# A hybrid decoder trunk on one core: the first phase laid out anew, with its loads in order of need, two modulation columns by matmuls, and a fixed engine order

## The chip, the cores and the metric

The program runs on one core of one Trainium2 chip. The metric is the device time of one execution, in microseconds (us), lower is better. The engines of the core work side by side, each through its own list of instructions in order: TensorE (PE in the profile, PEld for its weight loads) multiplies, VectorE (DVE) and ScalarE (ACT) do the elementwise work, SyncE (SP) issues nearly all transfers. They wait for one another through semaphores.

## What is computed

Two decoder layers over 512 tokens of width 1024. Each sub-layer is normalised and modulated by a shift and a scale that come from a conditioning vector `c`. The change touches only the start of layer 0: the modulation columns, the first norm, and the first projections that read its output.

```python
def rmsnorm(t, g):
    y = tf * lax.rsqrt(jnp.mean(tf * tf, axis=-1, keepdims=True) + EPS)
    return (y * g.astype(jnp.float32)).astype(t.dtype)

def modulate(t, g, shift, scale):
    return rmsnorm(t, g) * (1.0 + scale[:, None, :]) + shift[:, None, :]
...
c_act = jax.nn.silu(c)
for i in range(DEPTH):
    mod = c_act @ ada_w[i] + ada_b[i]
    sh1, sc1, g1, sh2, sc2, g2 = jnp.split(mod, 6, axis=-1)
    h = modulate(x, norm_mix[i], sh1, sc1)
    ...
        y = gla_mixer(h, gla_w_in[j], ...)      # proj = h @ w_in; q, k, v, r, glr
    x = x + g1[:, None, :] * y
    h = modulate(x, norm_ffn[i], sh2, sc2)
    x = x + g2[:, None, :] * swiglu(h, ffn_w_in[i], ffn_w_out[i])
```

## The kernel before

Activations lie transposed: eight tiles `x[k]` of 128 features by 512 tokens. A product is made in three matmuls (`mm3`, lines 172 to 177): both operands are split into a rounded high part and a low rest, and high times high, high times low and low times high are added up in PSUM. A weight unit of 128 by 1024 numbers is loaded into `raw` (line 155), copied to its high part `wh` by ScalarE (line 161), and VectorE makes the low part `wl` (line 169). The pool `wp` has three buffers each of `raw`, `wh` and `wl`.

A modulation column (128 of the 6144 outputs of `c_act @ ada_w`, `ada` at line 128) is made by VectorE: a tile `adaw` of 128 by 1024 weights is loaded (line 132), multiplied with `cact`, which holds silu(c) on every partition, and summed along the row (`junk`, line 136); the bias is added into `mod` (line 138). `gain` (line 143) makes the factor `gs` from a scale column. The pool for `adaw` has two buffers.

The first phase (lines 424 to 456) runs as follows.

- SP loads the eight tiles `x[k]`, with the row `crow` (the vector c) after the fourth. ScalarE's queue loads `kc` (an identity and a causal mask) and `cols` (biases and norm gains).
- TensorE spreads c over all partitions: two matmuls into `cb` (line 428) with one row of ones.
- ScalarE squares the `x[k]` (lines 261 and 264), VectorE adds the squares into `acc` (line 262). After the eighth square ScalarE makes `cact` from `cb` in two halves (line 434).
- `rstd_stats` (line 216): four matmuls with one output column each (`n_st`, line 225) sum `acc` over the partitions, and eleven small VectorE operations (lines 203 to 228, from `rs_v` to `rs_f`) make 1/rms. `rstd_spread` (line 234): four matmuls `n_bc` (line 240) bring it onto all partitions.
- `modulated` (line 267): `u` = x·gs·rstd on VectorE, `hh` = the rounded u + shift on ScalarE, `hl` the rest on VectorE.
- For each k the eight banks `ko` (the gate's small projection and seven of the eight head projections of q and k) receive 24 matmuls: 128 features of h[k] against the weight unit `gla_ko[k]`. All eight k make 192 matmuls, the phase's real work; the matmuls `gate` come behind them.

For k = 0 the order on TensorE, ScalarE and VectorE is written out by hand (`manual_schedule`). For k = 1 to 7 the framework's scheduler orders all engines, with one rule (line 450): the work of a column and weight unit k may not be issued before the low part `wl` of the unit before. SP's order is the scheduler's throughout. Each transfer also waits for the one eight transfers earlier on its queue of eight semaphores.

## Time and profile before

| What | Value |
|---|---|
| time, median of 3 runs | 1204.73 us (1204.16 to 1206.95) |
| the profiled execution, span from first to last instruction | 1203.1 us; the profile gives no other time for it |
| share of the span with a busy engine | PE 98%, weight loads 83%, DVE 61%, ACT 34% |
| instructions | 15359, of them 6010 matmul passes |
| DMA | 156.66 MB, mean 130 GB/s |
| first ten slices of the span (30.1 us each): PE busy, in tenths | 5 9 9 9 9 9 9 9 9 9 |
| the same for the DMA engines | 8 8 3 2 4 5 3 4 4 1 |

A busy share says little about a stage: matmuls are pipelined and their recorded ends overlap the next one's start. What ends last is read from the chain of waits, from the starts of successive instructions, and from what each engine's idle time ended with. The runs' median lies 1.6 us above the profiled span; what lies around the span is not resolved by the profile, so a difference worked out on the span is applied to the median as it stands. In the clock column of the table by stretches, 1.00 stands for full speed and 0.50 for half; it starts from the first event that the profiler recorded.

### The profile page before, as it was taken

How to read it: one execution, taken by the hardware profiler on the slowest of the kernel's cores; microseconds unless marked ns; L12 is line 12 of the kernel's file. 1: busy time of each engine (PE TensorE's matmuls, PEld its weight loads, DVE VectorE, ACT ScalarE, POOL GpSimd, SP SyncE). 2: the span in 40 equal slices, each digit the busy share in tenths (PEclk: the TensorE clock that was granted, in tenths of full speed). 3: DMA queues.
4: the chain of work that ended last, by engine and by line, in shares of the span. 5: the costliest groups of instructions: out<-in, count | busy, mean ns of one | idle time of the engine just before them, and what ended most of it. 6: DMA issues, size and time to landing. Idle time of an engine off the chain costs nothing.

```text
span 1203.1 us, 15359 instructions
## 1 busy us (share of the span) xinstructions
PE 1173.1 (98%) x6010; PEld 999.4 (83%) x6010; DVE 732.0 (61%) x1434; ACT 414.3 (34%) x652; POOL 15.9 (1%) x36
## 2 busy tenths in 40 slices
PE   5999999999999999999999999999999999999996
PEld 3788988899888888888899788989888888888886
DVE  6879788776665466846656778856433323333345
ACT  4271235343221223222334446634332223222331
POOL 0000000000000000000000022000000000000000
PEclk9999999999999999999999999999999999999998
DMA  8832453441574367547531123131333232333222
GB/s 283 266 98 105 170 179 127 134 160 53 193 262 142 113 243 251 152 158 246 182 114 45 57 66 106 35 124 34 96 98 103 91 103 85 92 105 105 83 76 71
DMA packets 47290, 156.66 MB, mean 130 GB/s; under 512 B 5601, under 2 KB 8033, under 8 KB 47218
## 3 DMA queue, kind: packets, MB, share of 16 engines
q1 hardware_dynamic: 45394, 153.38, 38.8%
q0 software_dynamic: 1536, 2.10, 0.8%
q8 instruction: 47, 0.77, 0.3%
q10 hardware_dynamic: 288, 0.21, 0.1%
q14 instruction: 25, 0.20, 0.1%
HBM read 151.47 MB, written 2.10 MB: 128 GB/s over the span
## 4 chain that ended last, share of the span: by engine, by line
PE 89%; DVE 6%; DMA 3%; ACT 1%; issue 1%; ACTq 0%; DVEq 0%
PE f L176 12%; PE f L177 12%; PE f L175 12%; PE op L175 9%; PE op L176 9%; PE op L177 9%; DMA adaw<-in_ada 2%; PE lv L541 2%; PE fg L176 2%; PE fg L177 2%; PE fg L175 2%; DVE junk L136 1%; PE v L175 1%; PE v L177 1%; PE v L176 1%; PE r L175 1%
## 5 line engine op out<-in xcount | busy, mean ns | idle before, releaser
L161 ACT CAST wh<-raw 128x1024 fp32r<-128x1024 f32 (+2 forms) x181 | 185.7, 1026 | 584.6 <-PE f L176 180.2
L169 DVE TENSOR_TENSOR wl<-raw,wh 128x1024 fp32r<-128x1024 f32 (+2 forms) x181 | 215.2, 1190 | 119.5 <-ACT wh L161 112.4
L175 PE MATMUL f<-hh,wh 128*128 128x512 f32 x640 | 249.2, 389 | 0.0
L176 PE MATMUL f<-hl,wh 128*128 128x512 f32 x640 | 249.2, 389 | 0.0
L177 PE MATMUL f<-hh,wl 128*128 128x512 f32 x640 | 249.2, 389 | 0.0
L175 PE MATMUL op<-acth,wh 128*128 128x512 f32 (+1 forms) x394 | 144.8, 368 | 0.0
L176 PE MATMUL op<-actl,wh 128*128 128x512 f32 (+1 forms) x394 | 144.5, 367 | 0.0
L177 PE MATMUL op<-acth,wl 128*128 128x512 f32 (+1 forms) x394 | 144.4, 367 | 0.0
L177 PEld LDWEIGHTS f<-hh,wl 128*128 128x128 f32 x640 | 120.1, 188 | 24.9
L176 PEld LDWEIGHTS f<-hl,wh 128*128 128x128 f32 x640 | 120.2, 188 | 24.9
L175 PEld LDWEIGHTS f<-hh,wh 128*128 128x128 f32 x640 | 120.1, 188 | 24.9
L136 DVE SCALAR_TENSOR_TENSOR junk<-adaw,cact 128x1024 bf16<-128x1024 f32 x96 | 117.1, 1220 | 12.7 <-DMA adaw<-in_ada 12.3
L284 DVE SCALAR_TENSOR_TENSOR x<-op,mod,x 128x512 f32<-128x512 f32 (+1 forms) x76 | 50.5, 665 | 119.2 <-PE op L177 119.1
L782 DVE TENSOR_TENSOR sg<-sg,f 128x512 f32<-128x512 f32 x40 | 27.5, 687 | 126.6 <-PE f L177 126.6
L176 PEld LDWEIGHTS op<-actl,wh 128*128 128x128 f32 x394 | 74.3, 189 | 12.2
L175 PEld LDWEIGHTS op<-acth,wh 128*128 128x128 f32 x394 | 74.3, 189 | 12.2
L177 PEld LDWEIGHTS op<-acth,wl 128*128 128x128 f32 x394 | 74.3, 189 | 12.1
L274 ACT ACTIVATE hh<-u,mod 128x256 fp32r<-128x256 f32 (+1 forms) x56 | 28.6, 536 | 56.5 <-DVE u L271 40.9
L262 DVE TENSOR_TENSOR acc<-acc,sq 128x512 f32<-128x512 f32 (+1 forms) x52 | 29.9, 576 | 17.5 <-ACT sq L261 17.2
L261 ACT ACTIVATE sq<-x 128x512 f32<-128x512 f32 (+1 forms) x45 | 23.6, 525 | 41.2 <-DVE x L284 38.5
L275 DVE SCALAR_TENSOR_TENSOR hl<-u,mod,hh 128x256 fp32r<-128x256 f32 (+1 forms) x56 | 27.9, 520 | 12.1 <-ACT hh L274 12.1
L784 DVE TENSOR_TENSOR actl<-sg,acth 128x512 fp32r<-128x512 f32 (+1 forms) x48 | 30.7, 641 | 0.8 <-ACT acth L783 0.5
(308 smaller groups left out, 1918.2 us busy)
## 6 DMA issues: line engine op xcount, KB each, us to landing
adaw<-in_ada SPq DMA_DIRECT2D x96, 512.0 KB, 4.1
raw<-in_ffn_in SPq DMA_DIRECT2D x80, 512.0 KB, 3.6
raw<-in_ffn_o SPq DMA_DIRECT2D x32, 448.0 KB, 3.3
raw<-in_ffn_o SPq DMA_DIRECT2D x16, 512.0 KB, 3.5
raw<-in_gla_ko SPq DMA_DIRECT2D x8, 512.0 KB, 4.5
raw<-in_gla_v SPq DMA_DIRECT2D x8, 512.0 KB, 3.6
raw<-in_gla_r SPq DMA_DIRECT2D x8, 512.0 KB, 3.6
raw<-in_gla_wo SPq DMA_DIRECT2D x8, 512.0 KB, 4.2
```

The source lines that it names most:

```text
L136: nc.vector.scalar_tensor_tensor(out=junk, in0=w, scalar=1.0, in1=cact, op0=ALU.mult, op1=ALU.mult, accum_out=acc)
L161: nc.scalar.copy(out=wh[:, :n], in_=raw[:, :n])
L169: ins = nc.vector.tensor_tensor(out=wl[:, :n], in0=raw[:, :n], in1=wh[:, :n].bitcast(F32), op=ALU.subtract)
L175: nc.tensor.matmul(ps, lhsT=ah, rhs=bh, start=start, stop=False)
L176: nc.tensor.matmul(ps, lhsT=ah, rhs=bl, start=False, stop=False)
L177: nc.tensor.matmul(ps, lhsT=al, rhs=bh, start=False, stop=stop)
L262: nc.vector.tensor_tensor(out=self.acc[:, c], in0=self.acc[:, c], in1=sq[:, c], op=ALU.add)
L274: nc.scalar.activation(out=hi[:, c], in_=u[:, c], func=AF.Identity, bias=sh)
L275: ins = nc.vector.scalar_tensor_tensor(out=lo[:, c], in0=u[:, c], scalar=sh, in1=hi[:, c].bitcast(F32), op0=ALU.add, op1=ALU.subtract)
L284: ins = nc.vector.scalar_tensor_tensor(out=x[k][:, c], in0=ps[:, c], scalar=mod[l][2 + 3 * j][:, k:k + 1], in1=x[k][:, c], op0=ALU.mult, o ...
L782: ins = nc.vector.tensor_tensor(out=sg[:, c], in0=sg[:, c], in1=pu[:, c], op=ALU.mult)
L784: nc.vector.tensor_tensor(out=lo[:, c], in0=sg[:, c], in1=hi[:, c].bitcast(F32), op=ALU.subtract)
```

## The change

It rewrites the first phase and leaves the rest of the program's instruction lists as they are, apart from the order of a few transfers just behind the phase.

- `crow` is loaded first, then the eight x, then for k = 0 and 1 the scale column, the shift column and the weight unit; in the loop, unit k+1 is requested at step k. SP's order is now written out too, for the whole phase.
- The sixteen `adaw` tiles of this phase land in a pool `first` of six buffers; the space is handed to the pool `att` behind the phase.
- TensorE begins with six matmuls `warm` of the identity against `kc`, whose result nobody reads.
- The two columns of k = 0 are made by TensorE (`ada_pe`): eight float32 matmuls of one output column each, from blocks that the host lays out transposed, against `ccol` (silu of c, one number a partition and block). The columns of k = 1 to 7 stay on VectorE.
- The eighth square is not added into `acc`; TensorE sums `acc` and the last `sq` in eight `n_st` matmuls.
- `cact` is made by ScalarE behind the fourth square and ahead of the fifth.
- For k = 1 to 7 the factor `gs` comes straight from the row sum in one operation, with `nb` = (1 + bias)·gain made once.
- TensorE, ScalarE and VectorE follow a written order for all eight k.

On TensorE, at the very start of the program (`am` is the bank of a column made by matmuls), before:

```order
L428 MATMUL cb<-crow,onesr 128x512 x2
L225 MATMUL n_st<-ones,acc 128x1 x4
L240 MATMUL n_bc<-kc,rs_f 128x128 x4
L447 MATMUL ko_230<-hh,wh 128x512
L447 MATMUL ko_231<-hh,wh 128x512
```

On TensorE at the same place, of the change:

```order
L453 MATMUL warm<-kc 128x256 x6
L456 MATMUL cb<-crow,onesr 128x512 x2
L226 MATMUL n_st<-ones,acc 128x1 x4
L226 MATMUL n_st<-ones,sq 128x1 x4
L477 MATMUL am<-ccol,adaw 128x1 x8
L241 MATMUL n_bc<-kc,rs_f 128x128 x4
L477 MATMUL am<-ccol,adaw 128x1 x8
L494 MATMUL ko_261<-hh,wh 128x512
```

Ten matmuls stood ahead of the first `ko`; now 36 do, and `cb` stands behind `warm`.

On ScalarE at the start of the program, before:

```order
L264 ACTIVATE acc<-x_83 128x512
L261 ACTIVATE sq<-x_84 128x512
L261 ACTIVATE sq<-x_85 128x512
L261 ACTIVATE sq<-x_86 128x512
L261 ACTIVATE sq<-x_87 128x512
L261 ACTIVATE sq<-x_88 128x512
L261 ACTIVATE sq<-x_89 128x512
L261 ACTIVATE sq<-x_90 128x512
L434 ACTIVATE cact<-cb 128x512 x2
```

On ScalarE at the same place, of the change:

```order
L265 ACTIVATE acc<-x_80 128x512
L262 ACTIVATE sq<-x_81 128x512
L262 ACTIVATE sq<-x_82 128x512
L262 ACTIVATE sq<-x_83 128x512
L468 ACTIVATE cact<-cb 128x512 x2
L262 ACTIVATE sq<-x_84 128x512
L262 ACTIVATE sq<-x_85 128x512
L262 ACTIVATE sq<-x_86 128x512
L470 ACTIVATE sq<-x_87 128x512
```

The two `cact` moved from behind the last square to ahead of the fifth.

On VectorE, from the end of the 1/rms chain (`rs_f`) into the first steps of the loop, before:

```order
L212 SCALAR_TENSOR_TENSOR rs_f<-rs_b,rs_o 128x4
L136 SCALAR_TENSOR_TENSOR junk,adac<-adaw,cact 128x1024
L138 TENSOR_TENSOR mod_0_109<-adac,cols 128x1
L271 SCALAR_TENSOR_TENSOR u<-x_83,gs_0_121,n_bc 128x512
L275 SCALAR_TENSOR_TENSOR hl<-u,mod_0_109,hh 128x512
L169 TENSOR_TENSOR wl<-raw,wh 128x1024
L136 SCALAR_TENSOR_TENSOR junk,adac<-adaw,cact 128x1024
L169 TENSOR_TENSOR wl<-raw,wh 128x1024
L138 TENSOR_TENSOR mod_1_110<-adac,cols 128x1
L136 SCALAR_TENSOR_TENSOR junk,adac<-adaw,cact 128x1024
```

On VectorE at the same place, of the change:

```order
L213 SCALAR_TENSOR_TENSOR rs_f<-rs_b,rs_o 128x4
L480 TENSOR_TENSOR mod_1_96<-am,cols 128x1
L147 SCALAR_TENSOR_TENSOR gs_0_107<-mod_1_96,cols 128x1
L480 TENSOR_TENSOR mod_0_95<-am,cols 128x1
L272 SCALAR_TENSOR_TENSOR u<-x_80,gs_0_107,n_bc 128x512
L276 SCALAR_TENSOR_TENSOR hl<-u,mod_0_95,hh 128x512
L170 TENSOR_TENSOR wl<-raw,wh 128x1024
L130 SCALAR_TENSOR_TENSOR junk,adac<-adaw,cact 128x1024
L499 TENSOR_SCALAR gs_0_107<-adac,cols,nb 128x1
L503 SCALAR_TENSOR_TENSOR u<-x_81,gs_0_107,rstd 128x512
L130 SCALAR_TENSOR_TENSOR junk,adac<-adaw,cact 128x1024
L139 TENSOR_TENSOR mod_0_95<-adac,cols 128x1
```

The row sum behind `rs_f` is gone; in its place the shift column `mod_0` waits for the second `am`, and `u` is queued behind it.

The diff, cut to its core (comments that it drops are left out):

```diff
+C_C = 148
+NC_COL = 156
...
-    att = ctx.enter_context(tc.tile_pool(name="att", bufs=2))
...
-    for k in range(KD):
-        nc.sync.dma_start(out=x[k], in_=t["x"][k])
-        if k == 3:
-            nc.sync.dma_start(out=crow[:1], in_=t["c"])
-    nc.scalar.dma_start(out=kc, in_=t["kc"])
-    nc.scalar.dma_start(out=cols, in_=t["cols"])
...
-    def ada(l, g, k):
-        n = g * KD + k
-        w = ap_.tile([P, D], F32, tag="adaw", name="adaw")
-        nc.sync.dma_start(out=w, in_=t["ada"][l * 48 + n])
+    def ada_load(l, g, k, pool):
+        w = pool.tile([P, D], F32, tag="adaw", name="adaw")
+        nc.sync.dma_start(out=w, in_=t["ada"][l * 48 + g * KD + k])
+        return w
+    def ada_dot(w):
         junk = ap_.tile([P, D], BF16, tag="junk", name="junk", bufs=1)
-        m = mod[l][g][:, k:k + 1]
         acc = sm.tile([P, 1], F32, tag="adac", name="adac")
         nc.vector.scalar_tensor_tensor(out=junk, in0=w, scalar=1.0, in1=cact,
                                        op0=ALU.mult, op1=ALU.mult, accum_out=acc)
+        return acc
+
+    def ada(l, g, k, w=None):
+        n = g * KD + k
+        m = mod[l][g][:, k:k + 1]
+        acc = ada_dot(ada_load(l, g, k, ap_) if w is None else w)
         nc.vector.tensor_tensor(out=m, in0=acc, in1=cols[:, C_ADAB + l * 48 + n:C_ADAB + l * 48 + n + 1],
                                 op=ALU.add)
...
-    with tc.manual_schedule(engines={PEM, ACTM, DVEM}):
-        cb = [bank("cb") for _ in range(2)]
-        for i in range(2):
-            nc.tensor.matmul(cb[i], lhsT=onesr, rhs=crow[:1, i * S:(i + 1) * S], start=True, stop=True)
-        nc.scalar.activation(out=cact[:, :1], in_=ones, func=AF.Silu)
-        ss = SumSq()
-        for k in range(KD):
-            ss.add(x[k])
-        for i in range(2):
-            nc.scalar.activation(out=cact[:, i * S:(i + 1) * S], in_=cb[i], func=AF.Silu)
-        ada(0, 1, 0)
-        gain(0, 0, 0)
-        y0 = rstd_stats(ss.acc, D, "n0")
-        w = wunit(t["gla_ko"][0], split_=False)
-        ada(0, 0, 0)
-        bc = rstd_spread(y0, None, "n0")
-        modulated(h[0], 0, 0, 0, bc)
-        nc.scalar.copy(out=rstd, in_=bc)
-        wunit_lo(w)
-        pko = [bank(f"ko{i}") for i in range(4)] + [abank(f"ko{i}") for i in range(4, 8)]
-        for n, (a, b) in enumerate(((0, 0), (0, 1), (1, 0))):
-            for i in range(8):
-                nc.tensor.matmul(pko[i], lhsT=w[a][:, i * P:(i + 1) * P], rhs=h[0][b], start=n == 0, stop=False)
-    for k in range(1, KD):
-        with tc.issue_after(last["w"]):
-            ada(0, 1, k)
-            ada(0, 0, k)
-            gain(0, 0, k)
-            w = wunit(t["gla_ko"][k])
-        modulated(h[k], k, 0, 0, rstd)
-        for i in range(8):
-            mm3(pko[i], sl(w, slice(None), slice(i * P, (i + 1) * P)), h[k], False, k == KD - 1)
+    def wload(src):
+        raw = wp.tile([P, 1024], F32, tag="raw", name="raw")
+        nc.sync.dma_start(out=raw, in_=src)
+        return raw
+
+    def wsplit(raw):
+        wh = wp.tile([P, 1024], F32R, tag="wh", name="wh")
+        wl = wp.tile([P, 1024], F32R, tag="wl", name="wl")
+        nc.scalar.copy(out=wh, in_=raw)
+        return wh, wl, raw
+
+    SPM = mybir.EngineType.SP
+    with tc.tile_pool(name="first", bufs=6) as first:
+        with tc.manual_schedule(engines={PEM, ACTM, DVEM, SPM}):
+            nc.scalar.dma_start(out=kc, in_=t["kc"])
+            nc.scalar.dma_start(out=cols, in_=t["cols"])
+            nc.sync.dma_start(out=crow[:1], in_=t["c"])
+            for k in range(KD):
+                nc.sync.dma_start(out=x[k], in_=t["x"][k])
+            ld = {}
+            for k in range(2):
+                ld[k] = ada_load(0, 1, k, first), ada_load(0, 0, k, first), wload(t["gla_ko"][k])
+            warm = abank("warm")
+            for i in range(6):
+                nc.tensor.matmul(warm[:, :256], lhsT=ident, rhs=kc, start=i == 0, stop=i == 5)
+            cb = [bank("cb") for _ in range(2)]
+            for i in range(2):
+                nc.tensor.matmul(cb[i], lhsT=onesr, rhs=crow[:1, i * S:(i + 1) * S], start=True, stop=True)
+            ccol = cst.tile([P, KD], F32, name="ccol")
+            nc.scalar.activation(out=ccol, in_=cols[:, C_C:C_C + KD], func=AF.Silu)
+
+            nb = cst.tile([P, KD], F32, name="nb")
+            nc.vector.scalar_tensor_tensor(out=nb, in0=cols[:, C_ADAB + KD:C_ADAB + 2 * KD], scalar=1.0,
+                                           in1=cols[:, C_NMIX:C_NMIX + KD], op0=ALU.add, op1=ALU.mult)
+            ss = SumSq()
+            for k in range(KD - 1):
+                ss.add(x[k])
+                if k == 3:
+                    for i in range(2):
+                        nc.scalar.activation(out=cact[:, i * S:(i + 1) * S], in_=cb[i], func=AF.Silu)
+            sq = R("sq")
+            nc.scalar.activation(out=sq, in_=x[KD - 1], func=AF.Square)
+            y0 = rstd_stats([ss.acc, sq], D, "n0")
+
+            def ada_pe(g):
+                w = ld[0][0 if g else 1]
+                am = abank("am")
+                for b in range(KD):
+                    nc.tensor.matmul(am[:, :1], lhsT=w[:, b * P:(b + 1) * P], rhs=ccol[:, b:b + 1],
+                                     start=b == 0, stop=b == KD - 1)
+                n = g * KD
+                nc.vector.tensor_tensor(out=mod[0][g][:, 0:1], in0=am[:, :1],
+                                        in1=cols[:, C_ADAB + n:C_ADAB + n + 1], op=ALU.add)
+
+            ada_pe(1)
+            gain(0, 0, 0)
+            w = wsplit(ld[0][2])
+            bc = rstd_spread(y0, None, "n0")
+            ada_pe(0)
+            modulated(h[0], 0, 0, 0, bc)
+            nc.scalar.copy(out=rstd, in_=bc)
+            wunit_lo(w)
+            pko = [bank(f"ko{i}") for i in range(4)] + [abank(f"ko{i}") for i in range(4, 8)]
+            for n, (a, b) in enumerate(((0, 0), (0, 1), (1, 0))):
+                for i in range(8):
+                    nc.tensor.matmul(pko[i], lhsT=w[a][:, i * P:(i + 1) * P], rhs=h[0][b], start=n == 0, stop=False)
+            for k in range(1, KD):
+                if k + 1 < KD:
+                    ld[k + 1] = ada_load(0, 1, k + 1, first), ada_load(0, 0, k + 1, first), wload(t["gla_ko"][k + 1])
+                wsc, wsh, raw = ld.pop(k)
+                nc.vector.tensor_scalar(out=gs_t[0][0][:, k:k + 1], in0=ada_dot(wsc),
+                                        scalar1=cols[:, C_NMIX + k:C_NMIX + k + 1], scalar2=nb[:, k:k + 1],
+                                        op0=ALU.mult, op1=ALU.add)
+                u = R("u")
+                nc.vector.scalar_tensor_tensor(out=u, in0=x[k], scalar=gs_t[0][0][:, k:k + 1], in1=rstd,
+                                               op0=ALU.mult, op1=ALU.mult)
+                w = wsplit(raw)
+                ada(0, 0, k, wsh)
+                sh = mod[0][0][:, k:k + 1]
+                hi, lo = h[k]
+                nc.scalar.activation(out=hi, in_=u, func=AF.Identity, bias=sh)
+                wunit_lo(w)
+                nc.vector.scalar_tensor_tensor(out=lo, in0=u, scalar=sh, in1=hi.bitcast(F32),
+                                               op0=ALU.add, op1=ALU.subtract)
+                for i in range(8):
+                    mm3(pko[i], sl(w, slice(None), slice(i * P, (i + 1) * P)), h[k], False, k == KD - 1)
+    att = ctx.enter_context(tc.tile_pool(name="att", bufs=2, reuse_waits="tile"))
...
+    for n in (0, KD):
+        d["ada"][n] = outer(aw[0][:, n * P:(n + 1) * P])[0]
+    put(C_C, f("c"))
```

## The prediction, made before the changed kernel was run

> **What bounds the kernel now.** I read the page first: PE is busy 98% of the span, and of its first ten slices only the first isn't full, so behind it the kernel runs at TensorE's own pace. A change to the first phase is worth what it moves the end of that phase. So I read the chain of waits from the start to the first `gate` (start, length, what):

> ```profile
> 11.04 0.64 ACT sq L261
> 11.71 0.70 DVE acc L262
> 12.46 1.88 PE n_st L225 x8
> 14.36 0.17 DVE rs_v L228
> ...
> 16.55 2.09 PE n_bc L240 x8
> 18.67 0.76 DVE u L271
> 19.45 0.73 ACT hh L274
> ...
> 38.40 6.28 DMA adaw<-in_ada
> ...
> 47.30 4.65 DMA adaw<-in_ada
> ...
> 53.23 4.50 DMA adaw<-in_ada
> ...
> 60.66 0.23 PE ko L177
> ...
> 70.20 0.23 PE ko L177
> 70.43 0.42 PE gate L175
> ```

> The phase has two parts. A head of one long dependence: last square, sum, `n_st`, eleven small operations, `n_bc`, `u`, `hh`. And a loop, where the chain runs through transfers of `adaw` again and again: two buffers are too few, and the column after next is requested only when one comes free. The last rows give TensorE's pace in the loop: 42 matmuls from 60.66 to 70.20, so 0.227 us each. The phase ends at 70.4. TensorE's timeline gives the loop's start:

> ```profile
> 6.18 3.75 PE L428 MATMUL cb<-crow,onesr 1*128 1x512 f32 x4 [6.18 <-DMA crow<-in_c]
> 20.22 3.78 PE L447 MATMUL ko<-hh,wh 128*128 128x512 f32 x8 [1.59 <-ACT hh L274]
> 23.80 2.12 PE L447 MATMUL ko<-hl,wh 128*128 128x512 f32 x8
> 25.76 1.97 PE L447 MATMUL ko<-hh,wl 128*128 128x512 f32 x8
> ```

> The loop lasts 70.4 − 20.2 = 50.2 us, and its 192 matmuls at 0.227 need 43.6. The reader should also see the first eight `ko` take 3.6 us (20.22 to 23.80) and the next eight 2.0: TensorE starts at half pace and doubles about 3.5 us later. So the whole head, `cb`, `n_st`, `n_bc`, ran at half pace, though the clock column says 1.00 there (it knows no event yet). The same small matmuls later in the program, at full pace:

> ```profile
> L225 PE MATMUL cq_st<-ones,acc x8: 249/250/271, 675.1 to 675.9; 128*128 128x1 f32 x8
> 681.90 1.13 PE L240 MATMUL cq_bc<-kc,rs_f 128*128 128x128 f32 x8
> ```

> Eight passes (a float32 matmul is two) start within 0.8 us: 0.11 a pass, against 1.88/8 = 0.23 in the head.

> **The change: the loop.** With six `adaw` buffers three columns' worth can be in flight, and each step needs three transfers of 512 KB. At the 358 GB/s of a well-filled stretch (its row stands below, at 102.57) that is 1.57 MB in 4.4 us, under the 5.45 of 24 matmuls. The requests lead: the scale column of k+3 goes out when that of k has been summed, some 14 us ahead of its use. So the starvation goes, and VectorE is late next. Its work for a step, by the starts in its timeline:

> ```profile
> 42.33 0.15 DVE L138 TENSOR_TENSOR mod<-adac,cols 128x1 f32<-128x1 f32 x1
> 42.40 1.22 DVE L169 TENSOR_TENSOR wl<-raw,wh 128x1024 fp32r<-128x1024 f32 x1
> 43.54 0.15 DVE L146 SCALAR_TENSOR_TENSOR gs<-mod,cols 128x1 f32<-128x1 f32 x1
> 43.73 0.75 DVE L271 SCALAR_TENSOR_TENSOR u<-x,gs,rstd 128x512 f32<-128x512 f32 x1
> 44.70 1.23 DVE L136 SCALAR_TENSOR_TENSOR junk<-adaw,cact 128x1024 bf16<-128x1024 f32 x1 [0.22 <-DMA adaw<-in_ada]
> 45.85 0.08 DVE L136 DVE_READ_ACCUMULATOR junk<-adaw,cact 128x1 f32 x1
> 45.96 0.16 DVE L138 TENSOR_TENSOR mod<-adac,cols 128x1 f32<-128x1 f32 x1
> 46.04 1.22 DVE L136 SCALAR_TENSOR_TENSOR junk<-adaw,cact 128x1024 bf16<-128x1024 f32 x1
> 47.18 0.08 DVE L136 DVE_READ_ACCUMULATOR junk<-adaw,cact 128x1 f32 x1
> 47.18 0.75 DVE L275 SCALAR_TENSOR_TENSOR hl<-u,mod,hh 128x512 fp32r<-128x512 f32 x1
> 47.85 0.15 DVE L138 TENSOR_TENSOR mod<-adac,cols 128x1 f32<-128x1 f32 x1
> ```

> Start to start, in the new order: `junk` 1.15, its sum to `gs` 0.11, `gs` 0.19, `u` 0.7, `junk` 1.14, sum to `mod` 0.11, `mod` 0.07, `wl` 1.14, `hl` 0.67: 5.3 us. That is just below TensorE's 5.45, so VectorE delays TensorE once, at k = 1, and never again: from the first `ko`, `hl(0)` ends at +0.7, `wl(0)` at +1.85, `hl(1)` at +7.15. The second matmul of k = 1 needs `hl(1)`; from there 23 + 6·24 = 167 matmuls take 37.9, and the last one's own time 0.2: the loop ends 45.4 us after its start, **4.8 us less** than the 50.2 of now. Whether k = 0 runs at half pace (7.05 us) or full (5.45) makes no difference, since `hl(1)` comes at 7.15. The one operation `gs` in place of two, and `nb`, lie within these 5.3; an `adaw` that came late by over 5 us would take the gain back.

> **The change: the head.** Now the costs. `cact` stands ahead of the fifth square on ScalarE and waits for `cb`, which stands behind `warm` on TensorE. Behind the waiting `cact` are four squares, and for these wait `acc`, `n_st` and all that follows. The rows for it:

> ```profile
> 4.28 0.23 DVE L459 CAST identr<-kc 128x128 fp32r<-128x128 f32 x1 [3.26 <-DMA kc<-in_kc]
> 9.19 1.27 ACT L261 ACTIVATE sq<-x 128x512 f32<-128x512 f32 x2 [1.15 <-DMA x<-in_x]
> 11.58 1.06 ACT L434 ACTIVATE cact<-cb 128x512 f32<-128x512 f32 x2
> ```

> `kc` is there at 4.3 and `warm` starts. A pass of 512 columns took 3.75/4 = 0.94, so twelve of 256 take 5.6 at half pace and `cb` 3.75: `cb` ends at E = 13.6 if the pace never doubles, and at 10.6 if it doubles 3.4 us behind the start of `warm`, as it did behind the start of `ko`. **I take E = 11.0**; bounds 10.0 (it doubles after 2.1 us) and 13.6. It was 9.9. Until then the x tiles have all landed (the last square began at 11.04). From E: the second half of `cact` 0.5, four squares of 0.64, and the seventh square's sum ends 0.3 behind the eighth: `n_st` starts at E+3.4, 14.4, where it was 12.46.

> What follows depends on TensorE's pace. `n_st` has 16 passes now (8 more for `sq`), each `am` 16. At half pace: `n_st` 1.90 as now plus 8·0.225 = 3.7, so `rs_v` at E+7.1; the eleven small ones as now (14.36 to 16.55) 2.2, to E+9.3. But the first `am` stands ahead of `n_bc` on TensorE, 3.6, to E+10.5, so `n_bc` starts only then, 1.8, to E+12.3. The second `am`, 3.6 and 0.2 to VectorE, to E+16.1; and `u` is queued behind the `mod_0` that waits for it. From `u` to the first `ko` 1.55 as now (18.67 to 20.22): the loop starts at **E+17.7 = 28.7**, 8.5 later than now. The two row sums that leave VectorE's head gain nothing: they ran under `n_st` and `n_bc`, and `u` was released by `n_bc` (18.67). Together +8.5 − 4.8 = **+3.7 us**. At full pace throughout (0.11 a pass) the same steps are 3.4 + 1.9 + 2.2 + 1.0 for `n_bc` + 2.0 for `am` + 1.55: the loop would start at E+12.0.

> So the question is whether TensorE keeps its pace from `warm` to `ko`. Rows of one-us stretches later in the program show when it is lost (PE, PEld, DVE, ACT, POOL, then granted clock, DMA share, GB/s):

> ```profile
> 686.00:687.00 1.00, 0.00 (x0) 0.00 (x0) 0.99 (x3) 1.00 (x2) 0.00 (x0) 1.00 0.00 0
> 687.00:688.00 1.00, 0.50 (x1) 0.19 (x1) 1.00 (x2) 1.00 (x3) 0.00 (x0) 1.00 0.00 0
> 688.00:689.00 1.00, 0.37 (x2) 0.33 (x3) 1.00 (x2) 1.00 (x3) 0.00 (x0) 1.00 0.14 15
> 689.00:690.00 1.00, 1.00 (x5) 0.86 (x4) 1.00 (x3) 0.24 (x1) 0.00 (x0) 0.83 0.83 246
> 690.00:691.00 1.00, 1.00 (x4) 0.72 (x4) 0.97 (x2) 0.00 (x0) 0.00 (x0) 0.50 0.33 132
> 693.00:694.00 1.00, 1.00 (x5) 0.76 (x4) 0.00 (x0) 0.00 (x0) 0.00 (x0) 0.96 0.00 0
> ```

> The clock halves at about 689.7 and is back at 693.1, 3.4 us later. The 3.4 us before the drop held 1.5 us of matmuls: a stretch less than half busy is enough to lose it. Between `cb` and `n_st` TensorE idles 3.4 us, so the clock should be lost near `n_st`. Does the row of small matmuls bring it back? `cb` streamed for 3.75 us at the start and did not (the `n_st` passes behind it took 0.23); it used one row of 128. A pass of `n_st` or `am` streams one column and for the rest loads weights. I take it that such passes count little, so half pace until `ko`.

> [...]

> **The rivals.**
> - Small passes do count, and the clock comes back in the middle of them. For it: 32 passes of 64 columns held it at full, with weights loaded all the time.

> ```profile
> 102.57:105.99 3.42, 3.42 (x34) 3.42 (x32) 3.42 (x8) 1.05 (x1) 0.00 (x0) 1.00 0.94 358
> ```

> Then `n_st` is slow and most of `am` fast; taking the doubling at E+7.5, the loop starts at E+13.8 = 24.8, 4.6 later: −0.2 us.
> - The other side: the clock is not lost at all, since the idle 3.4 us fall into two stretches each half busy. The loop starts at E+12.0, with an early doubling (E = 10.5) at 22.5: 2.3 − 4.8 = −2.5 us, −3.0 at E = 10.0. It decides in favour of the change once the loop starts before 22.6. Against it: the rows at 689.
> - The change doesn't do what it says: `warm` never doubles the pace, E = 13.6, start at 31.3: +6.3 us.
> - The loop still starves, on some wait of the written SP order: its 4.8 are not gained, +8.5.

> **How the numbers follow.** Chances: forecast 0.43, clock back midway 0.27, clock kept 0.20, `warm` without effect 0.06, starved loop 0.04. About 0.2%, 2.4 us, is what a measurement can tell here. Faster by more: 0.13 of the third case, 0.03 of the second, together 0.16. Slower by more: 0.39 of the first (the rest has E near 10), 0.01 of the second and the last two, 0.50. Within: 0.34. Applied to the median, 1204.7 + 3.7 = **1208.4 us**. The range goes from the third case near its better end, 1202.0, to half-way between forecast and `warm` without effect, 1210.0; outside lie about 0.05 below, and the starved loop and half the `warm` case above. Faster and same hold half the chance; the forecast's own range, E from 10.0 to 12.3, is 1207.4 to 1209.7.

> **What would show it.** In the changed profile: E in the end of `cb`; `cact` waiting for PE, then four squares without a gap; 16 passes of `n_st` at 0.22 (right) or 0.11 (wrong); `u` released by the `mod` of `am`; the first `ko` at 28.7; no DMA in the chain behind it; `gate` 45.4 after it. A first `ko` before 24 makes the prediction wrong, and so does a loop that takes under 44 or over 48.

## Result: 0.45% slower, at 1210.5 us, just above the range

| | median of its runs | ratio to before (95%) | profiled execution: time, span |
|---|---|---|---|
| before | 1205.52 us (1204.16 to 1206.95) | | span 1203.1 |
| changed | 1210.53 us (1209.58 to 1211.92) | 1.0045 (1.003 to 1.006) | 1209.58, 1207.8 |

The forecast was 1208.4 in a range of 1202.0 to 1210.0. The sign came true, and so did the mechanism within the first phase; what the forecast left out lies behind that phase. First the chain of waits of the changed kernel, from the start to behind the first phase (start, length, what):

```profile
2.78 5.14 PE warm L453 x12
7.92 1.92 PE cb L456 x4
9.87 0.60 ACT cact L468
10.46 0.53 ACT sq L262
...
13.35 3.58 PE n_st L226 x16
16.93 3.41 PE am L477 x16
20.34 1.92 PE n_bc L241 x8
22.25 3.22 PE am L477 x16
25.59 0.76 DVE u L272
26.37 0.73 ACT hh L275
27.14 7.68 PE ko L494 x24
...
72.90 0.42 PE gate L176
...
75.89 0.73 PE v L176
76.61 0.43 PE v L177
```

The head is on the chain as forecast: `warm`, `cb`, `cact`, squares, then 56 passes of `n_st`, `am` and `n_bc` at 0.20 to 0.24 each, where `n_st` and `am` take 0.11 in e7 below, so at half pace. The first `ko` starts at 27.14 (before 20.22). From there to `gate` no transfer is in the chain: the loop takes 45.7 us (50.1 before, from the starts 20.22 and 70.36 of TensorE's timeline). So the first phase ends 2.5 later. But the last two rows are new: behind `gate` a `v` matmul takes 0.43, where the pace of the loop was 0.227. The stretches of one us there (PE, PEld, DVE, ACT, POOL, granted clock, DMA share, GB/s), of the changed kernel:

```profile
75.00:76.00 1.00, 1.00 (x5) 0.55 (x4) 0.78 (x3) 1.00 (x3) 0.00 (x0) 0.85 0.00 0
76.00:77.00 1.00, 1.00 (x3) 0.81 (x4) 1.00 (x2) 1.00 (x3) 0.00 (x0) 0.50 0.68 131
78.00:79.00 1.00, 1.00 (x4) 0.71 (x4) 0.56 (x1) 0.99 (x2) 0.00 (x0) 0.50 0.01 0
79.00:80.00 1.00, 1.00 (x6) 0.81 (x5) 0.00 (x0) 1.00 (x3) 0.00 (x0) 0.94 0.00 0
```

and of before, at the same work:

```profile
72.00:73.00 1.00, 1.00 (x6) 0.77 (x5) 1.00 (x2) 1.00 (x3) 0.00 (x0) 1.00 0.00 0
74.00:75.00 1.00, 1.00 (x6) 0.82 (x5) 1.00 (x3) 1.00 (x2) 0.00 (x0) 1.00 0.71 270
```

TensorE is busy all the time in both, and yet the granted clock falls to half at 75.70 in the changed kernel, for 3.4 us. What stands ahead of it are the twelve `gate` matmuls, which use 16 of the 128 rows. The difference of the spans, 4.7, piece by piece from the starts in TensorE's timelines:

| stretch | before | changed | difference |
|---|---|---|---|
| start to first `ko` | 20.22 | 27.14 | +6.92 |
| to first `gate` | 50.14 | 45.69 | −4.45 |
| to first `v` | 2.96 | 2.99 | +0.03 |
| to the 25th `v` (24 each of `v`, `qk`, `lv`) | 13.61 | 15.17 | +1.56 |
| to first `qr`, to the end | 600.36, 515.81 | 600.87, 515.94 | +0.64 |

### The profile page after: what moved, and what is told of

Read it like the earlier page. It is cut to its first block, busy times and chain, and to the rows that moved or that the text cites. A ratio compares the mean times of both kernels' runs of the same rounds, so it can differ in the third digit from the quotient of the medians.

```text
span 1207.8 us, 15446 instructions
## 1 busy us (share of the span) xinstructions
PE 1183.9 (98%) x6062; PEld 1013.1 (84%) x6062; DVE 730.5 (60%) x1423; ACT 413.2 (34%) x652; POOL 15.9 (1%) x36
## 4 chain that ended last, share of the span: by engine, by line
PE 93%; DVE 5%; ACT 1%; DMA 1%; issue 0%; DVEq 0%; ACTq 0%
PE f L178 12%; PE f L177 12%; PE f L176 12%; PE op L176 9%; PE op L177 9%; PE op L178 9%; PE lv L600 2%; PE fg L177 2%; PE fg L178 2%; PE fg L176 2%; PE v L176 1%; PE v L178 1%; PE v L177 1%; PE ko L177 1%; PE ko L176 1%; PE ko L178 1%
## 5 line engine op out<-in xcount | busy, mean ns | idle before, releaser
L162 ACT CAST wh<-raw 128x1024 fp32r<-128x1024 f32 (+2 forms) x173 | 177.3, 1026 | 581.3 <-PE f L177 172.0
L177 PE MATMUL f<-hl,wh 128*128 128x512 f32 x640 | 249.0, 389 | 0.0
L177 PE MATMUL op<-actl,wh 128*128 128x512 f32 (+1 forms) x394 | 144.3, 366 | 0.0
L177 PEld LDWEIGHTS f<-hl,wh 128*128 128x128 f32 x640 | 120.1, 188 | 25.1
L178 PEld LDWEIGHTS f<-hh,wl 128*128 128x128 f32 x640 | 120.1, 188 | 24.8
L176 PEld LDWEIGHTS f<-hh,wh 128*128 128x128 f32 x640 | 120.1, 188 | 24.8
L130 DVE SCALAR_TENSOR_TENSOR junk<-adaw,cact 128x1024 bf16<-128x1024 f32 x94 | 114.8, 1222 | 11.0 <-DMA adaw<-in_ada 10.9
L177 PEld LDWEIGHTS op<-actl,wh 128*128 128x128 f32 x394 | 74.3, 189 | 12.3
L275 ACT ACTIVATE hh<-u,mod 128x256 fp32r<-128x256 f32 (+1 forms) x49 | 23.5, 509 | 38.5 <-DVE u L272 38.5
L262 ACT ACTIVATE sq<-x 128x512 f32<-128x512 f32 (+1 forms) x44 | 22.7, 521 | 38.6 <-DVE x L285 38.5
L842 ACT CAST acth<-sg 128x512 fp32r<-128x512 f32 (+1 forms) x48 | 28.1, 585 | 7.3 <-DVE sg L841 7.2
```

The source lines that it names most:

```text
L130: nc.vector.scalar_tensor_tensor(out=junk, in0=w, scalar=1.0, in1=cact, op0=ALU.mult, op1=ALU.mult, accum_out=acc)
L162: nc.scalar.copy(out=wh[:, :n], in_=raw[:, :n])
L176: nc.tensor.matmul(ps, lhsT=ah, rhs=bh, start=start, stop=False)
L177: nc.tensor.matmul(ps, lhsT=ah, rhs=bl, start=False, stop=False)
L178: nc.tensor.matmul(ps, lhsT=al, rhs=bh, start=False, stop=stop)
L842: nc.scalar.copy(out=hi[:, c], in_=sg[:, c])
```

## Experiments

All are built from the changed kernel. Theory A: the head costs what its waits and its passes at half pace cost, the loop gains by its buffers, and the 16-row `gate` loses the clock when it fills most of one window of the clock (3.41 us here, 75.70 to 79.11). In one table, from each profile, first what it gave:

| run | first `ko` | first `gate` | `gate` to 25th `v` | span | median | ratio (95%) |
|---|---|---|---|---|---|---|
| before | 20.22 | 70.36 | 16.57 | 1203.1 | | |
| changed | 27.14 | 72.83 | 18.16 | 1207.8 | 1210.53 | 1.0045 (1.003 to 1.006) |
| e1 columns on VectorE | 23.67 | 70.15 | 18.18 | 1206.4 | 1205.70 | 1.0009 (0.9999 to 1.0019) |
| e2 `cact` behind squares | 24.75 | 70.23 | 16.57 | 1203.8 | 1207.06 | 1.0014 (1.0005 to 1.0023) |
| e3 no `warm` | 25.48 | 70.97 | 19.73 | 1206.5 | 1208.53 | 1.0028 (1.0017 to 1.0040) |
| e4 `gate` padded | 26.86 | 72.31 | 16.19 | 1204.3 | 1206.99 | 1.0028 (1.0014 to 1.0043) |
| e5 loop alone | 19.70 | 66.32 | 18.17 | 1200.8 | 1201.42 | 0.9972 (0.9962 to 0.9982) |
| e6 loop, `gate` padded | 18.96 | 65.15 | 16.19 | 1197.7 | 1199.48 | 0.9961 (0.9947 to 0.9975) |
| e7 changed, gaps filled | 22.97 | 68.46 | 18.17 | 1203.8 | 1204.59 | 0.9998 (0.9989 to 1.0007) |
| e8 e6, gaps filled | 17.88 | 63.29 | 16.20 | 1194.9 | 1200.03 | 0.9959 (0.9945 to 0.9974) |
| e9 e8, `qr` gap filled | 18.08 | 63.49 | 16.20 | 1195.3 | 1199.12 | 0.9935 (0.9922 to 0.9948) |
| e10 e8, filled by 16 rows | 25.52 | 70.89 | 16.20 | 1205.4 | 1206.66 | 1.0005 (0.9994 to 1.0016) |
| e11 e8, filled by 64 rows | 25.97 | 70.85 | 16.20 | 1204.2 | 1208.95 | 1.0016 (1.0007 to 1.0025) |
| e12 changed again | 26.71 | 72.15 | 19.71 | 1207.5 | 1209.95 | 1.0034 (1.0022 to 1.0047) |
| e13 e4 again | 26.98 | 72.34 | 16.20 | 1203.7 | 1205.57 | 1.0010 (0.9996 to 1.0024) |

### One part of the head undone at a time: e1, e2, e3

e1, the columns of k = 0 as row sums on VectorE again:

```diff
-            ada_pe(1)
+            ada(0, 1, 0, ld[0][0])
...
-            ada_pe(0)
+            ada(0, 0, 0, ld[0][1])
```

> The change with one part undone: the two columns of k = 0 are made by VectorE again (two row sums), no am on TensorE; all else as changed. Theory A (the 32 half-pace am passes on TensorE, ahead of n_bc and of u, are the largest part of the longer head): n_st still starts near 13.4, n_bc directly behind rs_f at 19.1 instead of 20.2, u at 21.1, first ko at 22.7 instead of 27.1 (4.4 us earlier), gate 45.7 later at 68.4. Rival B (the head is set by the late n_st and the 1/rms chain, the am only fill idle time): first ko moves by less than 1.5 us. Behind the gate: if the clock's stretches of 3.41 us lie as in the changed run, the gate's twelve 16-row matmuls (68.4 to 71.4) fill most of one stretch and the clock drops again behind them.

The first `ko` comes 3.5 earlier, though `n_st` started 0.9 later than in the changed kernel (14.21 against 13.35: `warm` started 0.2 later, and, counted back 3.41 from the falls at 12.46 and 10.85, the clock came up only at 9.1, where it was 7.4; `cb` took 2.29 and 1.98). From `n_st` to `ko` it is 9.5 us where it was 13.8. So the two `am`, which the change took off VectorE, cost the head 4.3. The loop is 0.8 longer here, since `ko(0)` ran at half pace for longer (the clock came up at 29.54, 5.9 behind its start, against 31.33, 4.2 behind).

e2, `cact` behind the squares:

```diff
             for k in range(KD - 1):
                 ss.add(x[k])
-                if k == 3:
-                    (cact in two halves)
             sq = R("sq")
             nc.scalar.activation(out=sq, in_=x[KD - 1], func=AF.Square)
+            (cact in two halves)
```

> The change with one part undone: the two cact stand behind the last square on ScalarE again. Theory A (the fifth square waits for cb, which waits for warm): the squares follow the x tiles, n_st starts near 10.0 instead of 13.35, just behind cb, first ko near 23.5 (3.5 us earlier), gate near 69.2. Rival B (the x tiles or the sum would hold n_st anyway): n_st stays within 1 us of 13.35. Clock behind the gate: a gate from 69.2 to 72.2 would lie wholly in one stretch, so a drop is expected if the stretches lie as before.

`n_st` starts at 10.95 and the first `ko` at 24.75, 2.4 earlier than in the changed kernel. It was meant to be 23.5; the squares, no longer held up, follow each other from 6.36, right behind an x tile that landed, to 10.2, and VectorE's last sum ends at 10.9. These set the start of `n_st` then.

e3, without the six `warm`:

```diff
-            warm = abank("warm")
-            for i in range(6):
-                nc.tensor.matmul(warm[:, :256], lhsT=ident, rhs=kc, start=i == 0, stop=i == 5)
```

> The change without the six warm matmuls; cact still ahead of the fifth square. Theory A (the clock that warm raises is lost again at 10.8, before any matmul of the statistics; warm only delays cb): cb runs at half pace, 3.75 us, but starts when c is there (about 3 to 4.5), so it ends near 7.5 to 8.2 instead of 9.8; n_st starts near 11.3, first ko near 25.1, 2 us earlier, and n_st, am, n_bc take as long as in the changed kernel. Rival B (warm pays): first ko is later than 27.1.

`cb` runs from 2.37 to 6.1, `n_st` starts at 11.68, `ko` at 25.48: 1.7 earlier. So `warm` cost 1.7 and bought nothing, because the clock that it raises is lost at 10.85 again in the changed kernel, before `n_st` at 13.35. The three parts undone give 3.5, 2.4 and 1.7 at the first `ko`, and medians 4.8, 3.5 and 2.0 below the changed kernel's (4.3, 3.7 and 2.0 by the ratios, as they were run beside other runs of before). The two don't go hand in hand, and the clock's windows, which by its turns lie differently in each (`gate` starts 3.08, 1.67 and 0.84 us into one in e1, e2 and e3), are one reason: in the profiles e1 and e3 lose the clock behind `gate`, at 73.90 and 73.54, e2 doesn't (18.18, 19.73 and 16.57 to the 25th `v`).

### The loss behind `gate`: e4, e12, e13

The same head, with the operands of `gate` in tiles that were set to zero and used over all 128 rows:

```diff
+    for z in (gh, gl):
+        nc.gpsimd.memset(z.bitcast(F32), 0.0)
...
-            mm3(p_, (wgh[:RANK, c], wgl[:RANK, c]), (gh[:RANK], gl[:RANK]), True, True)
+            mm3(p_, (wgh[:, c], wgl[:, c]), (gh, gl), True, True)
```

> The change with one thing added: the gate's operands are padded with zero rows from 16 to 128, so that its twelve matmuls use all rows and give the same result in the same 2.9 us. Theory A (the clock is lost at 75.7 because matmuls of 16 of 128 rows count little): if rows alone count, no drop behind the gate, the first v matmuls run at 0.23 us instead of 0.43, end 1.7 us earlier, span about 1206. Rival B (what counts is the data that toggles, or the drop has another cause): the drop stays and the span is about 1207.8.

No loss behind `gate` any more (16.19 to the 25th `v`, against 18.16), at equal passes and columns; the added rows hold zeros, so here the rows in use made the difference, not what they hold. But its six runs lay in two groups, and so it was run again beside the changed kernel:

> The changed kernel as it is. Theory A (the forecast lacked the clock that is lost behind `gate`, 1.7 us in its profile, and the windows lie so that nearly every run loses it): median 1210 to 1211, mean clocks of 0.984 to 0.985 in most runs. Rival F (the four runs seen were by chance above the forecast): median 1208.4 to 1209.2.

> The kernel of e4, padded `gate`. Theory A: no loss behind `gate` in any run; median 1.7 to 2.2 below the changed kernel beside it, 1208 to 1208.8, so near the forecast of 1208.4 without that loss. Rival F: within 0.7 of the changed kernel beside it, the 3.5 of e4 then came from where else its clock held.

TensorE's timeline behind the phase, first of the changed kernel run again (e12):

```profile
72.15 0.49 PE L176 MATMUL gate<-glrh,wgh 16*128 16x512 f32 x1
...
76.03 0.63 PE L177 MATMUL v<-wl,hh 128*128 128x512 f32 x1
76.45 0.63 PE L178 MATMUL v<-wh,hl 128*128 128x512 f32 x1
76.88 0.63 PE L176 MATMUL v<-wh,hh 128*128 128x512 f32 x1
```

and of the padded one (e13):

```profile
72.34 0.39 PE L176 MATMUL gate<-glrh,wgh 128*128 128x512 f32 x1
...
75.29 0.39 PE L177 MATMUL v<-wl,hh 128*128 128x512 f32 x1
75.52 0.39 PE L178 MATMUL v<-wh,hl 128*128 128x512 f32 x1
75.74 0.39 PE L176 MATMUL v<-wh,hh 128*128 128x512 f32 x1
```

The same one-us stretch of both, e12 and then e13, shows the granted clock behind the engines' columns:

```profile
74.00:75.00 1.00, 1.00 (x6) 0.63 (x4) 0.93 (x2) 1.00 (x4) 0.00 (x0) 0.84 0.00 0
74.00:75.00 1.00, 1.00 (x6) 0.84 (x5) 1.00 (x2) 1.00 (x3) 0.00 (x0) 1.00 0.00 0
```

Start to start, 0.43 against 0.227. In e12 the clock was away for two windows, from 74.69 to 81.51, and `gate` to the 25th `v` took 19.71 against 16.20: 3.5 us. Of these 0.4 are not the clock's, since with 16 rows and no loss it is 16.57 (before, e2). The two traces make a clean pair: by the turns of the clock, `gate` starts 0.88 us into a window in e12 and 0.83 in e13, so the place of the windows doesn't tell them apart and the rows do. The median of e13 is 4.4 below that of e12 (2.9 by the ratios, since e13's runs again lie in two groups), more than the 1.7 to 2.2 that I expected, as I had sized the loss by a profile that lost one window only. All five runs of e12 and all four first ones have a mean clock of 0.984 or 0.985; of e13's twelve, eight have 0.987 or 0.988 and 1204.9 to 1206.0 us, four 0.985 or 0.986 and 1208.3 to 1211.5. Where those four lost their clock isn't known: the trace is of one of the eight. Rival F falls: the changed kernel came out at 1209.95 again.

### The loop by itself: e5, e6

The new loads and loop with the old head: no `warm`, `cact` behind the eighth square, all eight squares in `acc`, row sums on VectorE.

```diff
-            for k in range(KD - 1):
+            for k in range(KD):
                 ss.add(x[k])
...
-            y0 = rstd_stats([ss.acc, sq], D, "n0")
+            y0 = rstd_stats(ss.acc, D, "n0")
```

> The changed first phase keeps its six landing buffers, the order of loads and the rewritten loop, and loses the rest of its head: no `warm`, `cact` behind the squares, the eighth square summed into `acc` (8 passes of `n_st`), column 0 by row sums on VectorE. Theory A (the head costs what its waits and half-pace passes cost, and the loop gains by its buffers alone): `n_st` at 11.4, 8 passes of 0.23 to 13.3, `rs_f` 15.5, `n_bc` to 17.6, first `ko` 19.2, loop 45.7 as with the changed kernel, first `gate` 64.9; 5.5 us below before if the clock doesn't fall behind `gate`, 1199.4 (1201.1 if it does). Rival C (the loop runs without waits for transfers only because the long head gives the transfers 7 us more of a lead): TensorE waits for `adaw` or `raw` at k = 1, 2 or 3, the loop is 48 or longer, first `gate` at 67.5 or later, time 1202 or above.

> As e5, and the operands of `gate` zero-padded to 128 rows. Theory A: head and loop as e5 (first `ko` 19.2, `gate` 64.9), and no fall of the clock behind `gate` whatever the position of the windows, 1199.4; if e5 has the fall, e6 is 1.7 below it, otherwise within 0.5 of it. Rival C: as for e5, 1202 or above.

The loop keeps its gain with an early head: no wait for a transfer, first `gate` 4.0 earlier than before in e5 and 5.2 in e6. Rival C falls. In e5 that is 1.5 less than the 5.5 forecast: `n_st` came at 11.95 rather than 11.4, and `ko(0)` was at half pace until about 26 (the next 8 passes took 3.0 from 23.28), past the point where VectorE would have bound it. In the profiles e5 lost the clock behind `gate` (70.18 to 73.60) and e6 didn't, and their medians differ by 1.9, about what the loss of one window and the shorter padded `gate` gave in the profiles (18.17 − 16.19); but their intervals overlap.

### The clock as the cause of the slow passes: e7, e8, e10, e11

e7 is the changed kernel with TensorE's gaps filled by 15 matmuls whose result nobody reads; e8 the same on e6, with `warm` back:

```diff
+            def fill(ps, n):
+                for i in range(n):
+                    nc.tensor.matmul(ps[:, :256], lhsT=ident, rhs=kc, start=i == 0, stop=i == n - 1)
...
+            fill(warm, 8)
```

> The changed kernel whole, with 15 more matmuls of `kc` by `ident` (256 columns, all rows, results unread) in TensorE's gaps: 8 behind `cb`, 3 behind `n_st`, 1 behind `n_bc`, 3 behind the second `am`. Theory A (the head's small passes take 0.22 because the clock is at half): the clock stays up from 7.4 to `ko`; 16 passes of `n_st` 1.8, `am` 1.8 each, `n_bc` 1.05; `n_st` 13.4, first `am` to 18.3, `n_bc` to 19.3, second `am` to 21.5, first `ko` 23.2 at full pace, 3.9 earlier than the changed kernel: 1206.6 (1.7 less if the windows then spare `gate`). Rival D (a pass of one column costs 0.22 at either pace here, since it is bound by its weight load): `n_st` and `am` stay at 3.5 each, the fillers add 1.0 to 1.7, first `ko` 28 to 29, 1211.5 to 1212.

TensorE's timeline of e7 in the head (start, length, passes behind the x):

```profile
13.14 1.05 PE L226 MATMUL n_st<-ones,acc 128*128 128x1 f32 x8
14.05 1.03 PE L226 MATMUL n_st<-ones,sq 128*128 128x1 f32 x8
14.95 1.54 PE L457 MATMUL warm<-kc 128*128 128x256 f32 x6
16.32 1.84 PE L484 MATMUL am<-ccol,adaw 128*128 128x1 f32 x16
18.03 1.14 PE L241 MATMUL n_bc<-kc,rs_f 128*128 128x128 f32 x8
```

The passes take half of what they took (eight of `n_st` 0.91 from start to start, against 1.73), and the first `ko` is at 22.97, 4.2 earlier, although the fillers stand in the way. So the half pace was the clock's, and rival D falls. The kernel is now level with before; it still loses a window behind its 16-row `gate` (71.64 to 75.06).

> As e6, with `warm` kept ahead of `cb` and 11 fillers as in e7 (4 behind `cb`, 4 behind `n_st`, 3 behind `n_bc`). Theory A: `cb` 7.85 to 9.8 at full pace, `n_st` 11.4 to 12.3, `rs_f` 14.5, `n_bc` to 15.6, first `ko` 17.1, hl(1) 7.15 later, loop 45.7, `gate` 62.8: 7.5 below before, 1197.4, and 2.1 below e6. Rival D: `n_st` and `n_bc` at half pace, first `ko` 19.2 or later, same as e6. Rival C: the loop waits for transfers and gives the 2.1 back, same as e6 or above.

The head does as expected but for 0.8 (`n_st` at 11.95 where 11.4 was taken), and the profiled execution is 2.8 shorter than e6's. The median isn't lower than e6's: its six runs spread from 1196.7 to 1202.1.

The same with fewer rows, `lhsT=kc[:16, :P], rhs=kc[:16]` (and 64) in `warm` and the fillers:

> As e8, but `warm` and the fillers use 16 of the 128 rows (kc[:16] by kc[:16, :128]), with the same number of columns streamed. Theory A (a matmul counts for the clock by the rows it uses): the clock never comes up before `ko`: `warm` 12 passes of 0.43, `cb` 3.75 at half pace to 11.9, `n_st` behind 8 passes of fillers at 15.3, `n_bc` behind 8 more at 20.6, first `ko` 25.2, 7.3 later than in e8; 1206.5 to 1207.5. Rival B (streaming of columns counts, whatever the rows): all as in e8, first `ko` 17.9, 1200.

> As e10 with 64 rows. Counted by rows, the windows seen so far lost the clock at full-row work of 0.90, 1.15 and 1.5 us of 3.41 (behind `gate` in the changed kernel, in e3, and at 689 in before) and held it at 1.9 (e2). Theory A: `warm` fills a window with 1.7 us so counted, between the two, so either may come: first `ko` 17.9 (it counts) or 25.2 (it doesn't), nothing between but for one late doubling. Rival B: 17.9 as in e8.

e8, with 128 rows:

```profile
2.91 5.37 PE L453 MATMUL warm<-kc 128*128 128x256 f32 x12 [2.91 <-DMA kc<-in_kc]
8.21 1.98 PE L461 MATMUL cb<-crow,onesr 1*128 1x512 f32 x4
11.95 0.95 PE L226 MATMUL n_st<-ones,acc 128*128 128x1 f32 x8
17.88 2.11 PE L489 MATMUL ko<-hh,wh 128*128 128x512 f32 x8 [0.30 <-ACT hh L275]
```

e10, with 16:

```profile
2.92 5.48 PE L453 MATMUL warm<-kc 16*128 16x256 f32 x12 [2.92 <-DMA kc<-in_kc]
8.20 3.61 PE L461 MATMUL cb<-crow,onesr 1*128 1x512 f32 x4
15.16 1.86 PE L226 MATMUL n_st<-ones,acc 128*128 128x1 f32 x8
25.52 3.78 PE L489 MATMUL ko<-hh,wh 128*128 128x512 f32 x8
```

and e11, with 64:

```profile
2.78 5.49 PE L453 MATMUL warm<-kc 64*128 64x256 f32 x12 [2.78 <-DMA kc<-in_kc]
8.20 3.77 PE L461 MATMUL cb<-crow,onesr 1*128 1x512 f32 x4
```

With 16 rows TensorE streams without a pause from 2.9 to 25.5 and never comes to full pace; first `ko` 25.5, as forecast (25.2). Sixty-four rows weren't enough either (`cb` 3.77, first `ko` 25.97). Rival B, that streamed columns count whatever the rows, falls. The median of e11 lies 2.3 above that of e10, though their phases end alike (first `gate` 70.85 and 70.89); this is not explained.

### A gap further on: e9

In this kernel the filler function is named `topup`.

```diff
         run(kg)
+        topup(abank("fill"), 3)
         run(rope_group(0))
```

> As e8, and 3 more matmuls of `kc` by `ident` in TensorE's gap ahead of the first `qr` (680 in e8's profile, 686 to 689 in before), where before's profile loses the clock for 3.4 us. Theory A (e8's runs spread from 1196.7 to 1202.1 because the windows of the clock lie differently in each run, and most runs lose one there): the clock holds in the gap in all runs, mean clocks of 0.996 throughout, median 1197.5 (e8 1200.0). Rival E (the spread comes from elsewhere, transfers or other gaps): mean clocks still from 0.992 to 0.996, median 1199.5 to 1200.5.

The median is 1199.1, not 1197.5, and the mean clocks still reach from 0.993 to 0.997: theory A falls as it was stated, and rival E stands. The profile of e8 hadn't lost the clock in that gap to begin with, nor had those of e3, e4, e12 and e13, which have no filler there; all other traces but that of e9 itself had, between 683.16 (e6) and 693.52 (changed). Where the longer runs lose it stays open. e9 has the lowest ratio of all, 7.4 us below before, though its interval meets that of e8.

## Why the prediction was wrong

**What bounds the kernel.** The sentence "a change to the first phase is worth what it moves the end of that phase" is the step that failed: it puts all that follows the phase at nothing, and the time behind it wasn't fixed. The end moved by 2.5, less than the 3.7 forecast; in the profiles 2.2 came on behind it, and the median rose by 5.0. Behind the phase the clock's windows came to lie otherwise over the same `gate` matmuls. In before's profile the clock turns at 689.66 and 693.08, in the changed one at 10.85, 31.33, 75.70, 79.11, 693.52 and 696.92, which within each profile are whole multiples of 3.413 apart; I read these steps as the windows, also where the clock didn't turn. Counted back so, one ended at 71.85 in before, which cut the twelve `gate` in two, and each half shared its window with 1.9 us of `ko` or `v`. In the changed kernel the window from 72.29 to 75.70 held 0.54 of `ko` and else only `gate`: the clock fell, and the way to the 25th `v` took 1.56 longer. The padding shows the 16 rows as the cause of the fall (e13 beside e12), and e12 shows that two windows cost 3.1 (19.71 against 16.57). Both traces of the changed kernel have it. The prediction had the two rows that point to it, `cb` with one row of 128 that didn't raise the clock, and the drop after 1.5 busy us; it used them for the head alone.

That the shift of 2.5 us caused the loss is not shown, since where a window begins differed between two executions of one kernel: `gate` starts 0.54 us into one in the first trace of the changed kernel and 0.88 in the second. Before's trace, which kept the clock at `gate`, need not stand for all its runs either. Traces that lost one window behind the head have a mean clock of 0.995 (before, e6, e10, e11), those that lost two 0.993 or 0.994 (e3, e5, e7); of the 82 runs of before beside the experiments 45 have 0.993 or 0.994, so I estimate that about half of them lose a second window. The changed kernel's nine runs all have 0.984 or 0.985; its two traces have 0.985 and lost two behind the head. Why all nine do stays open, and before with a padded `gate` was not run. In e12's round the changed kernel was only 3.65 above before by the medians (1209.95 against 1206.30). That this is near the forecast +3.7 is luck: e12's phase ended 1.8 later, and two windows were lost behind it.

**E, 11.0 taken, 9.87 measured.** `kc` landed at 2.73, not at 4.3: the prediction read its time off a wait in before, where the transfers ahead of it were others. `warm` took 5.1 and `cb` then ran at full pace (1.98, against 3.75 in before), as supposed. ScalarE's wait is there:

```profile
9.01 0.60 ACT L468 ACTIVATE cact<-cb 128x512 f32<-128x512 f32 x1 [1.74 <-PE cb L456]
9.87 0.60 ACT L468 ACTIVATE cact<-cb 128x512 f32<-128x512 f32 x1 [0.26 <-PE cb L456]
```

**From E to the first `ko`, 17.7 forecast, 17.3 measured.** `n_st` at E+3.5 (3.4), `rs_v` at E+7.1 (7.1), first `am` done at E+10.3 (10.5), `n_bc` at E+12.2 (12.3), second `am` at E+15.6 (16.1). `u` waited for the `mod` of the second `am`:

```profile
25.50 0.16 DVE L480 TENSOR_TENSOR mod<-am,cols 128x1 f32<-128x1 f32 x1 [4.77 <-PE am L477]
25.59 0.75 DVE L272 SCALAR_TENSOR_TENSOR u<-x,gs,n_bc 128x512 f32<-128x512 f32 x1
```

So the choice of half pace was right, and so was the reason for it: 12 us of small passes, from 13.35 to 25.5, didn't bring the clock back, and e7 shows that it was the clock. The case of a clock that comes back midway and that of a clock never lost didn't occur; the latter is e7, made by force.

**The loop, 45.4 forecast, 45.7 measured** (−4.45 against −4.8; the forecast's own terms, 7.15, 37.9 and 0.2, add up to 45.25). VectorE's step was 5.4, not 5.3, as the new `gs` takes longer than the form it was priced by:

```profile
30.19 0.27 DVE L499 TENSOR_SCALAR gs<-adac,cols,nb 128x1 f32<-128x1 f32 x1
30.56 0.75 DVE L503 SCALAR_TENSOR_TENSOR u<-x,gs,rstd 128x512 f32<-128x512 f32 x1
```

It is 0.37 from its start to `u` here and 0.31 in the next steps, where 0.19 was taken. `hl(1)` ended at +7.2, as worked out, and the loop was TensorE's from there on. No transfer delayed it, in the changed kernel or in e5 to e9, where it starts up to 9 us earlier.

**The range** reached to 1210.0 for the sake of E alone. With the sum that the profile bears out, 2.5 for the phase and 2.2 behind it, 1204.7 + 4.7 = 1209.4 was to be expected, or 1210.2 from the median that before had beside the changed kernel (1205.5); the second term had no place in the bounds. Of these 2.2, 0.6 lies in the 1117 us behind the 25th `v`, and is not explained; the same stretch took from 1115.2 to 1118.3 in the fifteen traces.

## What to carry to other kernels

The time behind a changed stage wasn't fixed here: the clock's windows lay otherwise over it, from one kernel to the next and from one execution to the next (`gate` started 0.54 us into one, then 0.88). Look there for runs of matmuls with few rows (here 16 of 128), or for stretches like the one ahead of `qr` (1.5 us busy in 3.4), and put the loss of a window into the range: here one cost 1.6 us and two 3.1. Work given to an engine that ran at half pace cost double here (eight passes of `n_st` 1.73, against 0.91 in e7): either keep that engine fed with full-row matmuls up to the work that counts, as e8 does (first `ko` at 17.88, with 16 or 64 rows at 25.52 and 25.97), or leave the work where it was hidden. Measure the parts of a combined change apart: here the loads were worth some 4 us and the head cost 7.
